# Gate and up projections of 16 of a block's 22 chunks as seven products of quarters over normed activations

## The chip, the cores and the metric

The kernel runs on one core of a Trainium2 chip, in one launch. The metric is the time on the device in microseconds; the time before is 2031.37 us, the median of three runs (2030.7 to 2033.73).

## The reference, cut to what matters

A trunk of two layers over 512 tokens of width 1024, all in float32. Each layer is a feed-forward block, a mixer (layer 0: two kinds of attention, layer 1: a gated delta rule) and a second feed-forward block, so there are four feed-forward blocks. The change touches these:

```
def rms_norm(x, w):
    y = x * rsqrt(mean(x * x, axis=-1) + 1e-6)
    return y * w

def swiglu(h, w_gate, w_up, w_down):
    return (silu(h @ w_gate) * (h @ w_up)) @ w_down

x = x + 0.5 * swiglu(rms_norm(x, ffn_norm), w_gate, w_up, w_down)   # 512 x 1024; weights 1024 x 2816, 2816 x 1024
```

## The kernel before, in words

Activations lie transposed: `self.x` is eight tiles of 128 features by 512 tokens. Every float32 product is made of three matmuls on a high part and a low part of each operand (`mm3`, lines 179 to 183): high by high, high by low, low by high. A weight panel of 128 x 1024 is loaded from SP's queue (`panel`, line 170), its high part is a cast on ScalarE (line 174) and its low part a subtraction on VectorE (line 175). There are three buffers for raw panels and three each for high and low parts (`NRAW, NSPL`).

The norm is split. `prenorm` makes high and low parts of x times the gain (`self.xn`, line 250); the reciprocal root of each token is computed beside the first projections and stands as `self.rb`, the same row on all partitions (line 299). It is multiplied in behind the projection.

`ffn` (line 379) walks the 2816 hidden columns in 22 chunks of 128, in two blocks of 12 and 10. In a block it takes two chunks at a time: `proj_pair` for the gate and one for the up columns, each with two weight panels (half of K, 256 columns), into two PSUM tiles of 128 x 512. Behind it gate and up are each multiplied by rb on VectorE (lines 392, 396), the gate goes through silu on ScalarE, the product is formed (line 398) and split into a high and a low part (lines 226, 227), which stay in one of 14 `hid` tiles. After a block `add_out` multiplies its chunks by the rows of the down weights and adds half of the result to x (line 375). The last block of the network turns x to token order first (`to_tokens`) and adds there (`add_tok`).

Matmuls of the value projection in the attention layer (`proj_tok`, line 348) have 256 moving columns instead of 512, each with its own weight load.

The order on each engine is set by a planner at build time, which takes what is ready by its own model of time; on the chip each engine then works through its queue in that order. Tiles of one tag share a fixed number of buffers, and an instruction that writes a new one waits for the last reader of the old.

Of the kernel before, what the change touches and what calls it, by code (L numbers as in the profile page):

```python
# [10 lines left out]
F32 = mybir.dt.float32  # L11
F32R = mybir.dt.float32r
AF = mybir.ActivationFunctionType
ALU = mybir.AluOpType

P = 128
T = 512
D = 1024
KC = D // P
# [8 lines left out]
NRAW, NSPL = 3, 3  # L28
# [5 lines left out]
ORDER = (0, 1, 2, 3)  # L34
W_DIFF, W_SB = 2, 3
QD = 5
NHID = 14
HDPAD, HIDPAD = 112, 0
TANH = ((0, 0), (2, 0), (1, 1), (0, 1))
PLAN = (  # L40
    ("setup", 0, 3.5, 5), ("decays", 0, 22, 0), ("prep", 0, 25.5, 2.1), ("turned", 0, 43.5, 1.82),
# [60 lines left out]
class Trunk:  # L102
# [129 lines left out]
    def prenorm(self, gain, src=None, wait=1):  # L232

        nc = self.nc
        if src:
            self.xn = [[self.xp.tile([P, T], F32R, tag=f"xn{p}{c}", name=f"xn{p}{c}")
                        for p in "hl"] for c in range(KC)]
            for hf, half in enumerate(src):  # L240
                s = slice(hf * 256, (hf + 1) * 256)
                for c in range(KC):
                    h, l = self.xn[c]
                    self.split_to(h[:, s], l[:, s], half[c], gain[:, c:c + 1])
                    if c % 2:
                        nc.scalar.copy(out=self.x[c][:, s], in_=half[c])
                    else:
                        nc.vector.tensor_copy(self.x[c][:, s], half[c])
        else:
            self.xn = [self.split(self.xp, f"xnh{c}", f"xnl{c}", self.x[c], gain[:, c:c + 1])  # L250
                       for c in range(KC)]
        acc = self.np_.tile([P, T], F32, tag="acc", name="acc", bufs=1)
        nc.scalar.activation(acc, self.x[0], AF.Square)
        for c in range(1, KC):
            sq = self.np_.tile([P, T], F32, tag="sq", name="sq")
            nc.scalar.activation(sq, self.x[c], AF.Square)
            nc.vector.tensor_tensor(acc, acc, sq, op=ALU.add)
        self.pending = ([lambda: None] * wait
                        + [lambda: self.norm_cols(acc), lambda: self.norm_rows()])
# [117 lines left out]


    def ffn(self, wg, wu, wd, first=False, last=None):
        nc = self.nc  # L380
        with ExitStack() as st:
            pool = st.enter_context(self.tc.tile_pool(name="ffn", bufs=2))
            f0 = 0
            for size in (12, 10):
                hid = []
                for f in range(f0, f0 + size, 2):
                    g = self.proj_pair(wg, f * P, (self.a_ps, self.b_ps) if f == 2 else None,
                                       2 if first and f == 0 else 1)
                    u = self.proj_pair(wu, f * P, (self.a_ps, self.b_ps))
                    for j in range(2):  # L390
                        gr = pool.tile([P, T], F32, tag="gr", name="gr")
                        nc.vector.tensor_tensor(gr, g[j], self.rb, op=ALU.mult)  # L392
                        sg = pool.tile([P, T], F32, tag="sg", name="sg")
                        self.last_act = nc.scalar.activation(sg, gr, AF.Silu)
                        ur = pool.tile([P, T], F32, tag="ur", name="ur")
                        nc.vector.tensor_tensor(ur, u[j], self.rb, op=ALU.mult)
                        hd = pool.tile([P, T + HDPAD], F32, tag="hd", name="hd")[:, :T]
                        nc.vector.tensor_tensor(hd, sg, ur, op=ALU.mult)  # L398
                        slot = (f + j) % NHID
                        both = pool.tile([P, 2 * T + HIDPAD], F32R, tag=f"hid{slot}", name=f"hid{slot}",  # L400
                                         bufs=1)
                        h, l = both[:, :T], both[:, T:2 * T]
                        self.split_to(h, l, hd)
                        hid.append((h, l))
                if last is not None and f0 == 0:
                    self.to_tokens(pool)
                if last is None:
                    self.add_out(hid, wd, f0 * P, 0.5, (self.a_ps, self.a_ps, self.b_ps, self.b_ps))
                else:
                    self.add_tok(hid, wd, f0 * P, 0.5, f0 and self.finish(pool, *last))  # L410
                f0 += size

    def to_tokens(self, pool):
        nc = self.nc
        self.xt = []
        for b in range(NB):
            t = pool.tile([P, D], F32, name=f"xt{b}", bufs=1)
            for hf in range(2):
                ps = self.a_ps()
                for c in range(4):  # L420
                    nc.tensor.transpose(out=ps[:, c * P:(c + 1) * P],
                                        in_=self.x[hf * 4 + c][:, b * P:(b + 1) * P],
                                        identity=self.ident)
                nc.vector.tensor_copy(t[:, hf * 512:(hf + 1) * 512], ps)
            self.xt.append(t)
# [778 lines left out]
```

## Time and profile before

| | before |
|---|---|
| time, median of 3 runs | 2031.37 us (2030.7 to 2033.73) |
| profiled execution, its own time | 2032.96 us |
| its span | 2031.2 us |
| TensorE, VectorE, ScalarE, GpSimd busy | 1999.0, 1084.6, 748.3, 130.9 us |
| transfers | 192.24 MB, 95 GB/s |

The profile is of one execution. PE is TensorE's matmuls, PEld its weight loads, DVE VectorE, ACT ScalarE, POOL GpSimd; SPq and ACTq are queues that issue transfers. Line numbers are those of the kernel before. A row of the timeline has the start, the duration and what ran; matmuls are shown longer than the distance between their starts, since they are pipelined and their ends are modelled.

### The profile page before, as it was taken

Reading aid. Unit: us, or ns where it says so; the run is one execution under the profiler, and the core shown is the slowest. Engines: PE = TensorE matmul, PEld = TensorE weight load, DVE = VectorE, ACT = ScalarE, POOL = GpSimd, SP = SyncE. Lnnn points to the kernel's source line nnn. Section 1 sums busy time; section 2 is a strip of 40 time slices with the busy share of each in tenths; the row PEclk is TensorE's granted clock in tenths of the full one; section 3 lists DMA queues with packets and bytes.
Section 4 is the critical chain, followed back from the end, with each engine's and each line's share of the span. In section 5 each row is a group of like instructions: output and inputs, shape, how many; then the busy total and the mean of one; then the engine's idle time right before and its main releaser. Section 6 shows DMA issues by size and latency. Waiting matters only on the chain.

```text
span 2031.2 us, 24843 instructions
## 1 busy us (share of the span) xinstructions
PE 1999.0 (98%) x9786; PEld 1667.5 (82%) x9786; DVE 1084.6 (53%) x1752; ACT 748.3 (37%) x1359; POOL 130.9 (6%) x298
## 2 busy tenths in 40 slices
PE   8999999999999999999999999998999999999998
PEld 7888888889888888888888888877877788888887
DVE  6452454597675433444544344478577685443543
ACT  5232233355663222233332232355465453322322
POOL 0000000100000000000000000005432400000000
PEclk9999999999999999999999999999999999999999
DMA  4333333222123333333333333234223233223332
GB/s 157 94 99 98 94 99 98 86 84 73 47 90 103 94 104 94 94 103 94 94 95 102 94 95 103 93 111 115 77 80 92 75 100 104 94 90 97 93 101 76
DMA packets 189866, 192.24 MB, mean 95 GB/s; under 512 B 28546, under 2 KB 165044, under 8 KB 189748
## 3 DMA queue, kind: packets, MB, share of 16 engines
q1 hardware_dynamic: 158916, 182.62, 28.7%
q10 hardware_dynamic: 30832, 8.02, 1.7%
q8 instruction: 77, 1.26, 0.3%
q14 instruction: 41, 0.34, 0.1%
HBM read 185.35 MB, written 5.26 MB: 94 GB/s over the span
## 4 chain that ended last, share of the span: by engine, by line
PE 89%; POOL 5%; DMA 2%; DVE 1%; issue 1%; ACT 1%; ACTq 0%; SPq 0%; POOLq 0%
PE mm L181 10%; PE mm L182 10%; PE mm L183 10%; PE pa L181 9%; PE pa L183 8%; PE pa L182 8%; PE pb L181 8%; PE pb L183 8%; PE pb L182 8%; PE mm L96 4%; POOL tmp L1037 2%; POOL rr L1040 2%; PE pb L96 1%; DMA lb<-iud 1%; DMA iud<-iu 1%
## 5 line engine op out<-in xcount | busy, mean ns | idle before, releaser
L175 DVE TENSOR_TENSOR wl<-raw,wh 128x1024 fp32r<-128x1024 f32 (+1 forms) x348 | 413.2, 1187 | 564.1 <-ACT wh L174 563.1
L174 ACT CAST wh<-raw 128x1024 fp32r<-128x1024 f32 (+1 forms) x348 | 355.6, 1022 | 702.0 <-PE pb L182 279.9
L181 PE MATMUL mm<-xnh,wh 128*128 128x512 f32 (+1 forms) x816 | 316.5, 389 | 0.6 <-ACT wh L174 0.6
L183 PE MATMUL mm<-xnh,wl 128*128 128x512 f32 (+1 forms) x816 | 317.1, 389 | 0.0
L182 PE MATMUL mm<-xnl,wh 128*128 128x512 f32 (+1 forms) x816 | 316.7, 388 | 0.0
L181 PEld LDWEIGHTS mm<-xnh,wh 128*128 128x128 f32 x816 | 154.3, 189 | 31.6 <-ACT wh L174 1.0
L183 PEld LDWEIGHTS mm<-xnh,wl 128*128 128x128 f32 x816 | 154.2, 189 | 30.5 <-issue 0.5
L182 PEld LDWEIGHTS mm<-xnl,wh 128*128 128x128 f32 x816 | 154.3, 189 | 30.4 <-issue 0.2
L181 PE MATMUL pa<-xnh,wh 128*128 128x512 f32 x400 | 156.2, 390 | 0.0
L183 PE MATMUL pa<-xnh,wl 128*128 128x512 f32 x400 | 155.8, 389 | 0.0
L183 PE MATMUL pb<-xnh,wl 128*128 128x512 f32 x400 | 155.7, 389 | 0.0
L181 PE MATMUL pb<-xnh,wh 128*128 128x512 f32 x400 | 155.7, 389 | 0.0
L182 PE MATMUL pa<-xnl,wh 128*128 128x512 f32 x400 | 155.7, 389 | 0.0
L182 PE MATMUL pb<-xnl,wh 128*128 128x512 f32 x400 | 155.7, 389 | 0.0
L226 ACT CAST hid<-hd 128x512 fp32r<-128x512 f32 x88 | 54.5, 620 | 209.0 <-DVE hd L398 209.0
L96 PE MATMUL mm<-xnh,wh 128*128 128x512 f32 x256 | 109.2, 426 | 12.0 <-DVE cx L926 12.0
L392 DVE TENSOR_TENSOR gr<-mm,rb 128x512 f32<-128x512 f32 x80 | 55.2, 691 | 94.7 <-PE mm L183 94.6
L183 PE MATMUL pb<-hid,wl 128*128 128x512 f32 x264 | 102.8, 389 | 0.0
L181 PE MATMUL pa<-hid,wh 128*128 128x512 f32 x264 | 102.7, 389 | 0.0
L182 PE MATMUL pa<-hid,wh 128*128 128x512 f32 x264 | 102.7, 389 | 0.0
L183 PE MATMUL pa<-hid,wl 128*128 128x512 f32 x264 | 102.7, 389 | 0.0
L181 PE MATMUL pb<-hid,wh 128*128 128x512 f32 x264 | 102.7, 389 | 0.0
(308 smaller groups left out, 3365.1 us busy)
## 6 DMA issues: line engine op xcount, KB each, us to landing
raw<-in_ffn_w_gate_dram SPq DMA_DIRECT2D x88, 512.0 KB, 3.6
raw<-in_ffn_w_up_dram SPq DMA_DIRECT2D x88, 512.0 KB, 3.6
raw<-in_ffn_w_down_dram SPq DMA_DIRECT2D x88, 512.0 KB, 3.6
raw<-in_gdn_w_in_dram SPq DMA_DIRECT2D x32, 512.0 KB, 3.9
raw<-in_att_w_in_dram SPq DMA_DIRECT2D x24, 512.0 KB, 3.5
raw<-in_gdn_w_out_dram SPq DMA_DIRECT2D x16, 256.0 KB, 2.7
xr<-in_x_dram SPq DMA_DIRECT2D x4, 512.0 KB, 5.6
raw<-in_att_w_out_dram SPq DMA_DIRECT2D x4, 512.0 KB, 3.4
```

Of the source, the lines that this page charges most:

```text
L96: return self.tc.keep_in_program_order(self.engine.matmul(*args, **kw))
L174: nc.scalar.copy(out=h[:, :n], in_=raw[:, :n])
L175: nc.vector.tensor_tensor(l[:, :n], raw[:, :n], h[:, :n].bitcast(F32), op=ALU.subtract)
L181: self.te.matmul(out, lhsT=lh, rhs=rh, start=start, stop=False)
L182: self.te.matmul(out, lhsT=lh, rhs=rl, start=False, stop=False)
L183: self.te.matmul(out, lhsT=ll, rhs=rh, start=False, stop=stop)
L226: nc.scalar.copy(out=h, in_=src)
L392: nc.vector.tensor_tensor(gr, g[j], self.rb, op=ALU.mult)
L1037: nc.gpsimd.tensor_tensor(p, rr[:, :k, j:j + 1].broadcast_to(sh), lb[:, j, j + 1:].rearrange("p (o m) -> p o m", o=1) .broadcast_to(sh), o ...
L1040: nc.gpsimd.tensor_tensor(rr[:, :k, j + 1:], rr[:, :k, j + 1:], p, op=ALU.subtract)
```

## The change

In three of the four feed-forward blocks (all but the last) the 22 chunks are taken as 6, 8 and 8 instead of 12 and 10. The first six go as before (`eight`). Beside the down projection of these six, `quarters` multiplies x by gain and rb into normed activations, cuts them into quarters (half of K by half of the tokens) and keeps the high and low parts of the seven left operands, 28 tiles, in the tiles of `self.xn` and 12 more. The other 16 chunks go through `seven`, two chunks a time: the gate and up weights of the two chunks are cut into quarters (half of K by one chunk), and seven products of 256 tokens replace eight. Sums of quarters of weights come from transfers that add to what the tile holds (issued from GpSimd, `accum_op`) and from VectorE (t2, t4). Sums of products form partly in PSUM, where a second product adds to a first (X, Y, Z), partly on VectorE. The result is normed already, so the multiplications by rb fall away on this path. The hidden tiles are 10 instead of 14. The last block keeps 12 and 10 chunks and 14 tiles.

```diff
     def ffn(self, wg, wu, wd, first=False, last=None):
-        nc = self.nc
+        nc = self.nc
+        sizes, ring = ((12, 10), 14) if last is not None else ((6, 8, 8), 10)
         with ExitStack() as st:
             pool = st.enter_context(self.tc.tile_pool(name="ffn", bufs=2))
             f0 = 0
-            for size in (12, 10):
+            for size in sizes:
                 hid = []
                 for f in range(f0, f0 + size, 2):
-                    g = self.proj_pair(wg, f * P, (self.a_ps, self.b_ps) if f == 2 else None,
-                                       2 if first and f == 0 else 1)
-                    u = self.proj_pair(wu, f * P, (self.a_ps, self.b_ps))
-                    for j in range(2):
-                        gr = pool.tile([P, T], F32, tag="gr", name="gr")
-                        nc.vector.tensor_tensor(gr, g[j], self.rb, op=ALU.mult)
-                        sg = pool.tile([P, T], F32, tag="sg", name="sg")
-                        self.last_act = nc.scalar.activation(sg, gr, AF.Silu)
-                        ur = pool.tile([P, T], F32, tag="ur", name="ur")
-                        nc.vector.tensor_tensor(ur, u[j], self.rb, op=ALU.mult)
-                        hd = pool.tile([P, T + HDPAD], F32, tag="hd", name="hd")[:, :T]
-                        nc.vector.tensor_tensor(hd, sg, ur, op=ALU.mult)
-                        slot = (f + j) % NHID
-                        both = pool.tile([P, 2 * T + HIDPAD], F32R, tag=f"hid{slot}", name=f"hid{slot}",
+                    if f0 and last is None:
+                        inner = self.seven(pool, wg, wu, f)
+                    else:
+                        inner = self.eight(pool, wg, wu, f, first)
+                    for j, hd in enumerate(inner):
+                        slot = (f + j) % ring
+                        both = pool.tile([P, 2 * T], F32R, tag=f"hid{slot}", name=f"hid{slot}",
                                          bufs=1)
-                        h, l = both[:, :T], both[:, T:2 * T]
+                        h, l = both[:, :T], both[:, T:]
                         self.split_to(h, l, hd)
                         hid.append((h, l))
-                if last is not None and f0 == 0:
-                    self.to_tokens(pool)
+                if f0 == 0:
+                    if last is None:
+                        self.quarters(pool)
+                    else:
+                        self.to_tokens(pool)
                 if last is None:
                     self.add_out(hid, wd, f0 * P, 0.5, (self.a_ps, self.a_ps, self.b_ps, self.b_ps))
                 else:
                     self.add_tok(hid, wd, f0 * P, 0.5, f0 and self.finish(pool, *last))
                 f0 += size
+    def small(self, pool, tag):
+        n = T + HDPAD if tag == "hd" else T
+        return pool.tile([P, n], F32, tag=tag, name=tag)[:, :T]
+    def eight(self, pool, wg, wu, f, first):
+        nc = self.nc
+        g = self.proj_pair(wg, f * P, (self.a_ps, self.b_ps) if f == 2 else None,
+                           2 if first and f == 0 else 1)
+        u = self.proj_pair(wu, f * P, (self.a_ps, self.b_ps))
+        for j in range(2):
+            gr, sg, ur, hd = (self.small(pool, t) for t in ("gr", "sg", "ur", "hd"))
+            nc.vector.tensor_tensor(gr, g[j], self.rb, op=ALU.mult)
+            self.last_act = nc.scalar.activation(sg, gr, AF.Silu)
+            nc.vector.tensor_tensor(ur, u[j], self.rb, op=ALU.mult)
+            nc.vector.tensor_tensor(hd, sg, ur, op=ALU.mult)
+            yield hd
+    def quarters(self, pool):
+        nc = self.nc
+        tags = [(self.xp, f"xn{p}{c}") for c in range(KC) for p in "hl"]
+        tags += [(pool, f"sx{i}") for i in range(12)]
+        norm = []
+        for kh in range(2):
+            t = pool.tile([P, 4 * T], F32, tag="sr", name="xr")
+            for k in range(4):
+                c = kh * 4 + k
+                nc.vector.scalar_tensor_tensor(t[:, k * T:(k + 1) * T], self.x[c],
+                                               self.gain[:, c:c + 1], self.rb, ALU.mult, ALU.mult)
+            norm.append(t.rearrange("p (k t) -> p k t", k=4))
+        self.left = [[[], []] for _ in range(7)]
+        v2 = lambda t: t.rearrange("p (k t) -> p k t", k=2)
+        for i in range(2):
+            a = [[norm[kh][:, 2 * i:2 * i + 2, t * 256:(t + 1) * 256] for kh in range(2)]
+                 for t in range(2)]
+            s1, s2, s3, s4 = (v2(self.small(pool, t)) for t in ("gr", "sg", "ur", "hd"))
+            tt = nc.vector.tensor_tensor
+            tt(s1, a[1][0], a[1][1], op=ALU.subtract)
+            tt(s2, s1, a[0][0], op=ALU.subtract)
+            tt(s3, a[0][0], a[1][0], op=ALU.subtract)
+            tt(s4, a[0][1], s2, op=ALU.add)
+            for o, src in enumerate((a[0][0], s2, s1, s3, a[0][1], a[1][1], s4)):
+                h, l = (v2(pl.tile([P, T], F32R, tag=tag, name=tag, bufs=1))
+                        for pl, tag in (tags.pop(0), tags.pop(0)))
+                self.split_to(h, l, src)
+                self.left[o][0].append(h)
+                self.left[o][1].append(l)
+    def seven(self, pool, wg, wu, f):
+        nc = self.nc
+        x8 = lambda t: t.rearrange("p (x c) -> p x c", x=8)
+        def load(eng, v, kh, lo, hi, **kw):
+            for q, w in enumerate((wg, wu)):
+                eng.dma_start(v[:, q * 4:q * 4 + 4], w[kh * 512:(kh + 1) * 512,
+                                                       f * P + lo:f * P + hi]
+                              .rearrange("(k p) c -> p k c", p=P), **kw)
+        raw = lambda: x8(self.wp.tile([P, 1024], F32, tag="raw", name="raw", bufs=NRAW))
+        add = dict(accum_op=ALU.add)
+        b11 = x8(pool.tile([P, 1024], F32, tag="sb", name="sb"))
+        load(nc.sync, b11, 0, 0, P)
+        b2 = x8(pool.tile([P, 2048], F32, tag="sr", name="sr"))
+        load(nc.sync, b2, 1, 0, 2 * P)
+        t1, t3 = raw(), raw()
+        load(nc.sync, t1, 0, 0, P)
+        load(nc.gpsimd, t1, 0, P, 2 * P, **add)
+        load(nc.sync, t3, 0, P, 2 * P)
+        load(nc.gpsimd, t3, 1, P, 2 * P, **add)
+        b21, b22 = b2[:, :, :P], b2[:, :, P:]
+        X, Y, Z = self.mm_ps(), self.a_ps(), self.b_ps()
+        def product(ps, o, right, start=False):
+            h = x8(self.wp.tile([P, 1024], F32R, tag="wh", name="wh", bufs=NSPL))
+            l = x8(self.wp.tile([P, 1024], F32R, tag="wl", name="wl", bufs=NSPL))
+            self.split_to(h, l, right)
+            ah, al = self.left[o]
+            for q in range(2):
+                out = ps[:, q * 256:(q + 1) * 256]
+                for k in range(4):
+                    a = [t[k // 2][:, k % 2] for t in (ah, al)]
+                    for i, (wt, xt) in enumerate(((h, a[0]), (h, a[1]), (l, a[0]))):
+                        nc.tensor.matmul(out, lhsT=wt[:, q * 4 + k], rhs=xt,
+                                         start=start and q + k + i == 0,
+                                         stop=q == 1 and k == 3 and i == 2, skip_group_check=True)
+        def combine(tag, a, b, op):
+            t = self.small(pool, tag)
+            nc.vector.tensor_tensor(t, a, b, op=op)
+            return t
+        product(X, 0, b11, True)
+        p1 = self.np_.tile([P, T], F32, tag="acc", name="p1", bufs=1)
+        nc.scalar.copy(out=p1, in_=X)
+        t2 = raw()
+        nc.vector.tensor_tensor(t2, t1, b22, op=ALU.add)
+        product(Y, 1, t2, True)
+        u2 = self.np_.tile([P, T], F32, tag="sq", name="u2")
+        nc.vector.tensor_tensor(u2, p1, Y, op=ALU.add)
+        product(Z, 2, t1, True)
+        product(Y, 3, t3)
+        u3 = self.np_.tile([P, T], F32, tag="sq", name="u3")
+        nc.vector.tensor_tensor(u3, p1, Y, op=ALU.add)
+        c22 = combine("gr", Z, u3, ALU.subtract)
+        product(X, 4, b21)
+        t4 = raw()
+        nc.vector.tensor_tensor(t4, t2, b21, op=ALU.add)
+        product(Y, 5, t4)
+        c21 = combine("ur", p1, Y, ALU.add)
+        product(Z, 6, b22)
+        c12 = combine("ur", Z, u2, ALU.subtract)
+        for lo, hi in ((X, c21), (c12, c22)):
+            sg, hd = self.small(pool, "sg"), self.small(pool, "hd")
+            for i, c in enumerate((lo, hi)):
+                s = slice(i * 256, (i + 1) * 256)
+                self.last_act = nc.scalar.activation(sg[:, s], c[:, :256], AF.Silu)
+                nc.vector.tensor_tensor(hd[:, s], sg[:, s], c[:, 256:], op=ALU.mult)
+            yield hd
 
     def to_tokens(self, pool):
         nc = self.nc
```

## Rows read from the trace of the kernel before

**Rows 1.** The page, part 1: busy time, share of the span, instructions of each engine.
```profile
PE 1999.0 (98%) x9786; PEld 1667.5 (82%) x9786; DVE 1084.6 (53%) x1752; ACT 748.3 (37%) x1359; POOL 130.9 (6%) x298
```

**Rows 2.** The page, part 4: the chain that ended last, by engine.
```profile
PE 89%; POOL 5%; DMA 2%; DVE 1%; issue 1%; ACT 1%; ACTq 0%; SPq 0%; POOLq 0%
```

**Rows 3.** Busy time by stretch, the second feed-forward of layer 0 and what follows.
```profile
core 0: us, PE busy (x) PEld busy (x) DVE busy (x) ACT busy (x) POOL busy (x), PEclk, DMA share, GB/s
...
620.00:980.00 360.00, 360.00 (x1593) 298.16 (x1592) 161.22 (x191) 105.69 (x127) 1.87 (x1) 1.00 0.32 98
```

**Rows 4.** Timeline of TensorE, 512 columns: start, duration, what; 33 steps between.
```profile
140.12 0.39 PE L181 MATMUL pb<-xnh,wh 128*128 128x512 f32 x1
...
147.60 0.39 PE L181 MATMUL pa<-hid,wh 128*128 128x512 f32 x1
```

**Rows 5.** Timeline of TensorE, 256 columns, a projection's first and last of 96.
```profile
399.30 0.28 PE L181 MATMUL mm<-wh,xnh 128*128 128x256 f32 x1
399.30 0.19 PEld L182 LDWEIGHTS mm<-wl,xnh 128*128 128x128 f32 x1
...
410.69 0.28 PE L183 MATMUL mm<-wh,xnl 128*128 128x256 f32 x1
```

**Rows 6.** Groups by line: names, shapes, count | busy us, mean ns | idle before, releaser.
```profile
L175 DVE TENSOR_TENSOR wl<-raw,wh 128x1024 fp32r<-128x1024 f32 x324 | 396.7, 1224 | 557.6 <-ACT wh L174 556.6 <-DMA raw<-in_gdn_w_in_dram 0.4
L174 ACT CAST wh<-raw 128x1024 fp32r<-128x1024 f32 x324 | 340.7, 1052 | 677.1 <-PE pb L182 279.9 <-PE mm L182 149.3 <-issue 139.4
...
L227 DVE TENSOR_TENSOR hid<-hd,hid 128x512 fp32r<-128x512 f32 x88 | 60.8, 691 | 54.3 <-ACT hid L226 54.2
L398 DVE TENSOR_TENSOR hd<-sg,ur 128x512 f32<-128x512 f32 x88 | 60.5, 688 | 2.2 <-ACT sg L394 0.8
...
L394 ACT ACTIVATE sg<-gr 128x512 f32<-128x512 f32 x88 | 55.2, 628 | 128.7 <-DVE gr L392 128.7
L226 ACT CAST hid<-hd 128x512 fp32r<-128x512 f32 x88 | 54.5, 620 | 209.0 <-DVE hd L398 209.0
...
L396 DVE TENSOR_TENSOR ur<-pa,rb 128x512 f32<-128x512 f32 x44 | 30.4, 690 | 23.9 <-PE pa L183 23.9
L230 DVE SCALAR_TENSOR_TENSOR xnl<-x,norms,xnh 128x512 fp32r<-128x512 f32 x40 | 29.9, 753 | 0.4
...
L620 DVE TENSOR_TENSOR s<-pb,bias 128x256 f32<-128x256 f32 x8 | 3.3, 412 | 0.3 <-PE pb L617 0.3
```

**Rows 7.** Timeline of VectorE where the first block's down projection begins (147.60).
```profile
147.80 0.69 DVE L396 TENSOR_TENSOR ur<-pb,rb 128x512 f32<-128x512 f32 x1
148.70 1.23 DVE L175 TENSOR_TENSOR wl<-raw,wh 128x1024 fp32r<-128x1024 f32 x1 [0.21 <-ACT wh L174]
149.84 0.68 DVE L398 TENSOR_TENSOR hd<-sg,ur 128x512 f32<-128x512 f32 x1
```

**Rows 8.** Waits of SP's queue, 20 to 370 us: in total, times, longest.
```profile
SPq L170 <- DVE wl L175: 319.0, 64, 10.9
```

**Rows 9.** Transfers: issues, KB each, median us from issue to landing.
```profile
raw<-in_ffn_w_gate_dram SPq DMA_DIRECT2D x88, 512.0 KB, 3.6
...
lb<-iud ACTq DMA_DIRECT2D x16, 128.0 KB, 3.5
r<-rd ACTq DMA_DIRECT2D x8, 256.0 KB, 2.9
```

**Rows 10.** Waits of VectorE, 20 to 370 us: in total, times, longest.
```profile
DVE gr L392 <- PE mm L183: 23.6, 18, 2.0
DVE hid L227 <- ACT hid L226: 13.7, 20, 0.7
DVE ur L396 <- PE pa L183: 6.0, 10, 0.6
```

More of the change, by code (lines that the diff above doesn't have):

```diff
@@ L36 @@
 QD = 5
-NHID = 14
-HDPAD, HIDPAD = 112, 0
+HDPAD = 112
 TANH = ((0, 0), (2, 0), (1, 1), (0, 1))
@@ L232, in prenorm @@
     def prenorm(self, gain, src=None, wait=1):
-        nc = self.nc
+        nc, self.gain = self.nc, gain
         if src:
```

## The prediction

> **What bounds the kernel now.** I read the engine line of the page first [rows 1]: TensorE is busy 1999.0 of 2031.2 us, VectorE 1084.6, ScalarE 748.3, GpSimd 130.9. Then the chain that ended last [rows 2]: 89% of it is TensorE, so whatever shortens TensorE's stream shortens the kernel, until another engine's queue is late. Then the feed-forward stretches alone [rows 3]: TensorE is busy without a gap at full granted clock (1.00, the 2.4 GHz level), VectorE 161.2 of 360 us, the transfers take 0.32 of their engines' time at 98 GB/s. The busy time of one matmul is no price, since matmuls overlap in the record; the price is the distance between starts. For 512 columns [rows 4] 33 steps take 147.60 - 140.12 = 7.48 us, 0.2267 us each. For 256 columns, which the value projection of the attention layer already uses with a new weight load for each, the 96 matmuls of one projection [rows 5] have 95 steps in 410.69 - 399.30 = 11.39 us, 0.1199 each. That is more than half of 0.2267 (0.1133): halving a matmul costs 6%, and the change halves them.
>
> **TensorE's part of the change.** A pair of chunks (256 gate and 256 up columns) costs 2 projections x 2 x 8 x 3 = 96 matmuls of 512 columns now: 96 x 0.2267 = 21.76 us. By seven products it costs 7 x 2 x 4 x 3 = 168 of 256 columns: 168 x 0.1199 = 20.14 us. The gain is 1.62 us a pair (7.4%, where seven eighths would be 12.5%). Three of the four blocks take this path, eight pairs each: 24 x 1.62 = 38.9 us. The down projection keeps its matmuls, 6 + 8 + 8 chunks in place of 12 + 10.
>
> The Trainium skill (TensorE: Matmul & The Clock Gate, Back-to-back issue gap) prices a lone warm gap at the columns over 2.4 GHz plus 2.5 ns, 215.8 and 109.2 ns; as an estimate this would make a pair 20.72 and 18.35 us and the gain 24 x 2.37 = 57 us. The trace disagrees with both gaps (227 and 120 ns), and with the same section's 131 ns for a sustained stream of 512 columns; the measured gaps decide, and the sum stays at 38.9.
>
> **VectorE beside a pair.** Durations from [rows 6]. It now makes seven low parts of 1024 columns instead of four, adds two sums t2 and t4 of that size (9 x 1.224 = 11.0 us), five combinations of 512 that read PSUM (5 x 0.690 = 3.5), four products of 256 (nearest the 256-column addition, 4 x 0.412 = 1.6) and two low parts of the hidden tiles (2 x 0.691 = 1.4): 17.5 us in 20.14. The multiplications by rb behind the projections are gone. Back to back the pieces overlap a little (148.70 to 149.84 is 1.14 us for a piece shown with 1.23 [rows 7]), about 0.08 on each of 20 pieces, so 15.9 to 17.5 us, 79 to 87%. ScalarE: seven casts of 1.052, a copy and two casts of 0.620, four halves of a 0.628 activation at most: 11.7 us. Both fit. What is behind whom: with three buffers for high and low parts, the parts of a product can be made once the third product before it is done; two products, 2 x 24 x 0.1199 = 5.75 us, cover one cast and one subtraction of 2.28, which leaves 3.4 us of slack for VectorE's order. Product four writes the bank that u2 has read, with one product (2.88 us) in between. I charge 0.3 us a pair, 7.2 in all: bounds 0 (the gapless stretches now) and 1.4 (rival A).
>
> **The transfers.** A pair loads 2 MiB now and 3.5 MiB then: four operands of 0.5 MiB in 512-byte rows, the second half of K whole (1 MiB), and t1 and t3 brought by an accumulating transfer each. 3.67 MB in 20.14 us is 182 GB/s; by the 0.32 share for 98 GB/s [rows 3] that is 0.59 of the engines' time, if accumulating costs as loading does. Issued from SP: eight a pair instead of four; SP now waits for VectorE to give buffers back (319.0 us in 64 waits of one block, [rows 8]), so loads start early enough with room left. The accumulating ones stand on GpSimd's queue, which has nothing else in these stretches; each waits for the plain load before it. This is the part that no row shows. One tile needs two of 256 KB. Lower end: both at once as one 512 KB load, 3.6 us; upper end: in turn at the rate of the slowest load, 128 KB in 3.5 us, so 14.0 [rows 9]. I take the 256 KB load in 512-byte rows, twice in turn, 5.8 us, since its rows are of the same size. The cover: t1 of the next pair gets its buffer when t4 has been made, some 3.5 us after a pair's start (the low part of product two at 2.3, then t4), and the parts of the next pair's product one must be ready 8 x 2.88 = 23.0 us after that start. Taking off the sum t2, a cast and a subtraction (3.5), 16.0 us are left for the load (3.6) and the accumulation. 5.8 fits; above 12.4 TensorE waits even with perfect order.
>
> **The quarters.** Once a block VectorE makes eight normed tiles (0.753), eight sums (0.688) and 14 low parts (0.691), 6.0 + 5.5 + 9.7 = 21.2 us, and ScalarE 14 casts, 8.7 us. They stand beside the down projection of six chunks, 144 x 0.2267 = 32.6 us, with that projection's six panels (7.3), the rest of the last pair (ur, hd and two hidden parts, 4.1), four updates of x (2.8) and the first parts of the seven products (4.9): 40.3 us, 7.7 too many. But the order is not the program's: at 148.70 a panel of the down projection is split between pieces of an earlier pair [rows 7], so ready work is moved ahead, and the normed tiles need only x and rb, known early in the block. Without them the overhang is 1.7. I charge 2 us a block, 6 in all (0 to 24). The eight further updates of x a block, 5.5 us, lie beside the down panels, where VectorE is under half busy; without that cover 16.5 us.
>
> **Sum.** The profiled execution took 2032.96 us, 1.6 over the median of 2031.37. 2032.96 - 38.9 + 7.2 + 6.0 = 2007.3; beside the median 2005.7, so I say **2006 us**. Own range 1992 (no stalls) to 2026 (quarters at 24, pairs at 0.3 and a little more).
>
> **Rivals.** A: VectorE becomes the bound. For it: its queue is in order, and in a block it now waits 23.6 + 13.7 + 6.0 us for TensorE and ScalarE beside panels [rows 10], over 11 pairs 3.9 us a pair. 17.5 + 3.9 = 21.4 us, gain 0.3 a pair, 8 in all, less the quarters: 2030. Against: much of that waiting is for work that isn't due. 18%; it goes from 2024 to 2038.
>
> B, slower: an accumulating transfer lands late at the head of VectorE's queue. t2 waits for it there, and u2, u3 and the low parts of products in progress stand behind it. The planner places t2 by its own idea of that transfer; what lands over 3.4 us after its place stops TensorE, every pair. The gain is gone at a wait of 1.37 us a pair (1.62 less a block's 2 us over eight), 4.8 us late. With the transfer at 10.6 us, between the 5.8 taken and the 14.0, and a place chosen by 3.6, it is 7.0 late: 3.6 us of wait, pair 23.74, 24 x 1.98 + 6 = 54 slower, 2085; at 14.0 it is 2167. For it: no accumulating transfer or GpSimd issue is in the trace. Against: the 16.0 us of cover. 24%.
>
> The Trainium skill (Collectives: The Full Stack, The bandwidth ceiling) says that an adding transfer runs at half the rate because it needs two source reads; as an estimate 7.2 us for 512 KB. No run here shows it; by it the tile lands 3.6 us late and the wait is 0.2 us, still a gain.
>
> C: a matmul of 256 columns doesn't keep its pace. The weight load is shown with 0.19 us; if it bound, a pair would take 168 x 0.19 = 31.9 us and the kernel 243 more, 2275. [rows 5] are against it: 0.1199 with a load each. 2%.
>
> **How the numbers follow.** Forecast 56%, A 18%, B 24%, C 2%. About 0.2% (4 us) is what can be told from no change. Faster: 55 of the forecast and 5 of A, 0.60; same: 9 of A, 1 of the forecast, 1 of B, 0.11; slower: 4 of A, 23 of B, 2 of C, 0.29. The range 1990 to 2062 holds nearly all of the forecast and A and some two fifths of B, about 82%.
>
> **What would show it.** Steps of 0.12 us between the 256-column matmuls and 20.1 to 20.5 us from one pair to the next would show the main term; TensorE gaps inside pairs, ended by VectorE's low parts, rival A; VectorE's t2 waiting for the accumulating transfer, rival B, with the landing times of the transfers issued from GpSimd as its measure. Gaps in the down projection of the first six chunks would price the quarters. The forecast is wrong if pairs take over 21.4 us, or if the transfers' share passes 0.9.

## The result, and the profile after

The changed kernel takes **2076.86 us** (median of 4 runs, 2076.05 to 2081.11) against 2031.89 for the kernel before on the same chip: a ratio of **1.0225, 95% interval 1.0207 to 1.0242**. It is 45 us slower; the forecast was 26 us faster, with a range that ended at 2062. The profiled execution took 2081.11 us, 48.1 over the one of before.

The page of the changed kernel answers to [rows 1] and [rows 2]: the span, the busy times, two DMA queues (packets, MB, share of 16 engines' time; q0 carries the accumulating transfers), the chain that ended last.

```profile
span 2079.3 us, 29425 instructions
...
PE 1992.8 (96%) x11514; PEld 1741.8 (84%) x11514; DVE 1302.3 (63%) x2058; ACT 897.7 (43%) x1577; POOL 256.0 (12%) x394
...
q1 hardware_dynamic: 209604, 195.21, 30.7%
q0 software_dynamic: 50688, 25.17, 9.9%
...
PE 53%; DMA 6%; POOL 5%; DVE 3%; issue 2%; ACT 1%; ACTq 0%; DVEq 0%; POOLq 0%; SPq 0%
```

The 53% can't be set beside the 89% of before. The shares of this chain add up to some 70% of the span, because it could be followed back only to 607.6 us; of the part followed, about three quarters are TensorE's. What the chain does show is DMA: 6% of the span, about 8% of the part followed, where it was 2%. TensorE now waits, and behind the wait stands a transfer. Nor has TensorE's busy time fallen by the 39 us of the sum: 1999.0 to 1992.8. ScalarE's has risen by 149 us; 41 of these (32 loads of activation tables, below) are in no term of the sum.

The waits of the changed kernel (engine and tile, what ended the wait: us in all, times, longest):

```profile
DVE raw L511 <- DMA raw<-in_ffn_w_up_dram: 70.5, 21, 5.3
...
PE pa L498 <- DVE u L518: 38.2, 17, 3.8
```

L511 is the sum t2, L518 the combination u3, L498 the seven products. VectorE waits at t2 for an accumulating transfer, and TensorE waits for u3. The chain of waits links the two, in one pair of the second layer (start, duration, what):

```profile
755.94 2.88 PE mm L498 x24
...
762.74 1.24 DVE wl L226
...
763.98 0.68 POOL raw L471
764.65 0.08 issue
764.73 5.90 DMA raw<-in_ffn_w_up_dram
...
770.80 1.23 DVE raw L511
772.03 0.61 DVE u L518
772.64 0.14 issue
772.77 4.61 PE pa L498 x24
```

And VectorE's timeline of the same pair (line 522 is the sum t4, which gives back the buffer that t1 of the next pair takes):

```profile
759.07 1.22 DVE L522 TENSOR_TENSOR raw<-raw,sr 128x1024 f32<-128x1024 f32 x1
...
765.62 1.22 DVE L226 TENSOR_TENSOR wl<-raw,wh 128x1024 fp32r<-128x1024 f32 x1 [1.66 <-ACT wh L225]
770.80 1.23 DVE L511 TENSOR_TENSOR raw<-raw,sr 128x1024 f32<-128x1024 f32 x1 [3.96 <-DMA raw<-in_ffn_w_up_dram]
771.95 0.68 DVE L518 TENSOR_TENSOR u<-p,pa 128x512 f32<-128x512 f32 x1
```

The t2 at 770.80 belongs to the **next** pair, whose product two begins at 783.12, 12 us on. In VectorE's queue it stands ahead of this pair's u3. Its operand lands at 770.63, VectorE stands idle for 3.96 us, and u3, which needs product four, is made only at 771.95, 4.5 us after the last matmul of that product began (767.41). Product six writes the bank that u3 reads, so TensorE stops between products five and six.

Windows of the changed kernel around that stop, and over the attention layer (busy us of each engine, then PEclk, DMA share, GB/s; the share counts the whole time of every packet that starts in the window, so it can pass 1 in a short one):

```profile
core 0: us, PE busy (x) PEld busy (x) DVE busy (x) ACT busy (x) POOL busy (x), PEclk, DMA share, GB/s
386.50:636.50 250.00, 236.45 (x1331) 202.78 (x1330) 174.25 (x376) 168.87 (x333) 9.82 (x12) 0.97 0.23 71
...
734.60:824.30 89.70, 84.27 (x674) 83.75 (x673) 63.22 (x76) 39.29 (x53) 15.63 (x12) 0.96 0.70 158
...
767.20:770.20 3.00, 3.00 (x27) 2.93 (x25) 0.00 (x0) 1.05 (x1) 1.99 (x2) 1.00 1.30 159
770.20:772.80 2.60, 0.16 (x3) 0.06 (x1) 2.00 (x3) 1.33 (x2) 0.00 (x0) 1.00 1.30 161
772.80:777.40 4.60, 4.60 (x26) 4.60 (x27) 3.36 (x5) 0.47 (x2) 0.00 (x0) 0.63 0.57 176
777.40:780.20 2.80, 2.80 (x25) 2.80 (x25) 2.25 (x3) 1.32 (x2) 0.00 (x0) 1.00 0.98 277
```

A second price shows here. After 2.4 us of idling, the granted clock of the next 4.6 us is 0.63 on the mean, mostly the 1.2 GHz level, and product six takes 4.61 us where the others take 2.88. By the starts of the 24 matmuls behind each of the 18 stops, 11 were followed so (4.3 to 5.3 us), 7 were not (2.9).

**Where the time went.** I measured the six stretches of four pairs (672 matmuls each) from the starts of their matmuls. At 0.12 us a step each is 80.63 us, 483.8 in all, where the old path takes 6 x 4 x 21.76 = 522.2. After the change they take 88.57, 95.33, 89.71, 90.47, 90.90 and 90.59, 545.6 in all. The excess of 61.8 us is 42.3 of gaps (one in each of the first three pairs of a stretch, steps of 1.1 to 4.1 us, mean 2.5) and 19.5 of longer steps behind them. The attention layer, read apart from the pairs that follow it, takes 250.1 us in place of 228.0: 22.1 more. The projections before and after it, in the other layers, differ by some 2 us. Together -38.4 + 61.8 + 22.1 + 2 = +47.5, of the 48.1 seen.

The attention layer is a cost of its own. ScalarE's groups there, by line:

```profile
L813 ACT ACT_TABLE_LOAD x14 | 18.0, 1283 | 0.2
...
L823 ACT ACT_TABLE_LOAD x9 | 11.5, 1283 | 0.2
...
L812 ACT ACT_TABLE_LOAD x5 | 6.4, 1283 | 0.1
```

These are 28 loads of activation tables of 1.283 us, 36 us of ScalarE, at the exponentials (812, 823) and the logarithm (813); the whole kernel has 40 loads, and had 8. (The expectation below counts 29, with one at line 623.) The same stretch before, in a window of that kernel:

```profile
376.10:604.00 227.90, 227.90 (x1330) 199.02 (x1329) 175.06 (x381) 132.03 (x305) 10.92 (x19) 1.00 0.23 73
```

The same matmuls, gapless then; now TensorE idles 13.5 us and ScalarE has 37 us more. The other 8.6 of the 22.1 us are TensorE's busy time (236.45 in place of 227.90), at a granted clock of 0.97 in place of 1.00: here too the stops are followed by slower matmuls. The timeline of ScalarE at the end of the block before shows where it starts:

```profile
338.50 0.41 ACT L531 ACTIVATE sg<-gr 128x256 f32<-128x256 f32 x1
338.92 1.28 ACT L187 ACT_TABLE_LOAD   x1
...
341.29 1.28 ACT L531 ACT_TABLE_LOAD   x1
342.58 0.42 ACT L531 ACTIVATE sg<-ur 128x256 f32<-128x256 f32 x1
```

Line 187 loads a table that holds both exponential and logarithm, pinned behind `self.last_act`, the last silu that the program wrote. On the new path that is c22's, which is ready before those of c21 and c12 (`ur`). So the load goes in at 338.92, a late silu at 341.29 brings its own table back, and from then on the attention layer fetches a table at many changes between exponential and logarithm.

### The profile page after: what moved, and what is told of

Read it like the earlier page. It is cut to its first block, busy times and chain, and to the rows that moved or that the text cites. A ratio compares the mean times of both kernels' runs of the same rounds, so it can differ in the third digit from the quotient of the medians.

```text
span 2079.3 us, 29425 instructions
## 1 busy us (share of the span) xinstructions
PE 1992.8 (96%) x11514; PEld 1741.8 (84%) x11514; DVE 1302.3 (63%) x2058; ACT 897.7 (43%) x1577; POOL 256.0 (12%) x394
## 3 DMA queue, kind: packets, MB, share of 16 engines
q0 software_dynamic: 50688, 25.17, 9.9%
## 4 chain that ended last, share of the span: by engine, by line
PE 53%; DMA 6%; POOL 5%; DVE 3%; issue 2%; ACT 1%; ACTq 0%; DVEq 0%; POOLq 0%; SPq 0%
PE pa L498 5%; PE pa L182 5%; PE pa L180 5%; PE pa L181 5%; PE pb L182 5%; PE pb L180 5%; PE pb L181 5%; PE mm L95 4%; DMA raw<-in_ffn_w_up_dram 4%; PE pb L498 3%; PE mm L498 3%; PE mm L181 3%; PE mm L180 3%; PE mm L182 3%; POOL tmp L1159 2%; POOL rr L1162 2%
## 5 line engine op out<-in xcount | busy, mean ns | idle before, releaser
L174 DVE TENSOR_TENSOR wl<-raw,wh 128x1024 fp32r<-128x1024 f32 (+1 forms) x252 | 295.5, 1173 | 275.2 <-ACT wh L173 274.4
L173 ACT CAST wh<-raw 128x1024 fp32r<-128x1024 f32 (+1 forms) x252 | 254.3, 1009 | 425.6 <-PE pb L181 153.5
L180 PE MATMUL mm<-xnh,wh 128*128 128x512 f32 (+1 forms) x432 | 169.3, 395 | 7.7 <-DVE qT L660 5.6
L182 PE MATMUL mm<-xnh,wl 128*128 128x512 f32 (+1 forms) x432 | 169.9, 394 | 0.0
L181 PE MATMUL mm<-xnl,wh 128*128 128x512 f32 (+1 forms) x432 | 168.8, 391 | 0.0
L226 DVE TENSOR_TENSOR wl<-raw,wh 128x1024 fp32r<-128x1024 f32 x96 | 117.5, 1224 | 73.2 <-ACT wh L225 73.2
L471 POOL DMA_DIRECT2D raw<-in_ffn_w_gate_dram x48 | 67.8, 1412 | 698.0 <-DMA raw<-in_ffn_w_gate_dram 330.0
L498 PE MATMUL pa<-xnh,wh 128*128 128x256 f32 x288 | 87.0, 302 | 39.5 <-DVE u L518 38.2
L498 PE MATMUL pa<-sx,wh 128*128 128x256 f32 x576 | 118.0, 298 | 0.0
L181 PE MATMUL pb<-hid,wh 128*128 128x512 f32 x264 | 102.7, 389 | 0.0
L180 PE MATMUL pb<-hid,wh 128*128 128x512 f32 x264 | 102.2, 389 | 0.0
L95 PE MATMUL mm<-xnl,wh 128*128 128x512 f32 x256 | 101.8, 398 | 0.0
L95 PE MATMUL mm<-xnh,wl 128*128 128x512 f32 x256 | 101.7, 397 | 0.0
L498 PEld LDWEIGHTS pa<-sx,wh 128*128 128x128 f32 x576 | 97.5, 208 | 0.0
```

Of the source, the lines that this page charges most:

```text
L95: return self.tc.keep_in_program_order(self.engine.matmul(*args, **kw))
L173: nc.scalar.copy(out=h[:, :n], in_=raw[:, :n])
L174: nc.vector.tensor_tensor(l[:, :n], raw[:, :n], h[:, :n].bitcast(F32), op=ALU.subtract)
L180: self.te.matmul(out, lhsT=lh, rhs=rh, start=start, stop=False)
L181: self.te.matmul(out, lhsT=lh, rhs=rl, start=False, stop=False)
L182: self.te.matmul(out, lhsT=ll, rhs=rh, start=False, stop=stop)
```

## The experiments

My theory: the two losses are independent. The first: t2 at the head of VectorE's queue holds u3, through its place and not through a lack of room on VectorE. The second: the table load, pinned behind the wrong silu, costs the attention layer 22 us. The rivals: VectorE is simply too full (A of the prediction); the transfers are too slow, so that no order helps; and, for the attention layer, the extra traffic or the shifted schedule.

**The table load behind all four silus.** `acts` takes the place of `last_act` at both silus.

```diff
-        self.tc.add_manual_dep(ld.ins, self.last_act.ins.name, dep, reason="tables")
+        for act in self.acts[-4:]:
+            self.tc.add_manual_dep(ld.ins, act.ins.name, dep, reason="tables")
```

> The attention layer's stretch became 22 us longer although none of its code changed: ScalarE loads its activation tables 29 times there instead of once (1.283 us each, 36 us more of ScalarE). Theory: the table load of that layer waits for the activation that the program issues last in the feed-forward block, and on the new path this is no longer the one that runs last, so a silu behind it brings its own table back. Here the load waits for the last four silus; nothing else changes. My theory: at most two loads in that layer's stretch, TensorE's idle time of 13.5 us there gone, 22 us less, 2055 (2050 to 2060); the stretches of seven products stay at 88 to 95 us. Rival (the layer is late because of buffers or transfers left over from the block before): loads go, time stays within 5 us of 2077.

Measured: 2061.60 us (2057.58 to 2065.7, 4 runs), ratio 1.0147 (1.0130 to 1.0164). The kernel's loads fall from 40 to 10, and the part from the start of the attention layer to the down projection behind it from 315.4 to 293.7 us, 21.7 less. One load is left in that layer, and it stands behind the last silu (ScalarE's timeline of this kernel):

```profile
347.96 0.41 ACT L533 ACTIVATE sg<-ur 128x256 f32<-128x256 f32 x1
348.39 1.28 ACT L188 ACT_TABLE_LOAD   x1
```

The second theory holds, and nothing else moved on VectorE and TensorE: both have the same instructions in the same order as in the changed kernel. The time fell by only 15.3 us, to 1.6 above the 2060 that I had allowed. In this profile the six stretches came out 4.5 us longer (550.1), which the edit does not explain, and its runs spread over 8 us; the profiled execution of the changed kernel was also the slowest of its four, 4.3 us over their median.

**Without the accumulating transfers.**

```diff
-        load(nc.gpsimd, t1, 0, P, 2 * P, **add)
...
-        load(nc.gpsimd, t3, 1, P, 2 * P, **add)
```

> Left out: the accumulating transfers, so that t1 and t3 hold one quarter of the weights each instead of a sum. Everything else is issued as before. Theory (the accumulating transfer lands late and what stands behind it on VectorE stops TensorE): the gap of 1.1 to 4.1 us in three of four pairs goes, and with it the half clock behind it; a stretch of four pairs takes 81 to 83 us instead of 88.6 to 95.3, in all some 58 us less, 2019 (2010 to 2028). Rival A (VectorE has too much work): stretches stay above 87 us, time above 2060.

Measured: 2017.76 us, ratio 0.9931 (0.9917 to 0.9946). All six stretches take 80.63 us, without a gap; the attention part stays at 315.4. The order of the instructions on TensorE, VectorE and ScalarE is that of the changed kernel; only the transfers are gone. So VectorE has room for everything that the pairs give it, and rival A falls. What is left adds up: 2031.5 - 38.4 + 22.1 + 2 = 2017.2.

**t2 behind the previous pair's u3.** Nothing is taken away; the edit has two entries of VectorE's queue change places.

```diff
-        nc.vector.tensor_tensor(t2, t1, b22, op=ALU.add)
+        with self.tc.issue_after(self.u3) if self.u3 else nullcontext():
+            nc.vector.tensor_tensor(t2, t1, b22, op=ALU.add)
...
-        nc.vector.tensor_tensor(u3, p1, Y, op=ALU.add)
+        self.u3 = nc.vector.tensor_tensor(u3, p1, Y, op=ALU.add).ins
```

> Only the order of two instructions on VectorE changes: the next pair's sum t2, which waits for the accumulating transfer, goes behind u3 instead of ahead of it, in three of four pairs. Same work, same transfers. Theory (head of the queue): u3 is done on time, product six of seven starts without a gap, the clock stays; the tile still lands before product one of the next pair needs it. Stretches 81 to 84 us, 2022 (2012 to 2035). Rival (the chain of load and accumulation is too long whatever the order): the gap moves to the next pair's first products, time above 2060. Rival A (too much work on VectorE): also above 2060.

Measured: 2035.67 us (10 runs), ratio 1.0020 (1.0011 to 1.0030): 41 us back from the 2076.86, yet just above the range that I expected. The stretches take 83.1 to 83.8 us (500.6 in all). The gap at product six is gone. Smaller ones, steps of 0.56 to 1.4 us, stand in product seven: ahead of its first matmul, and a little later where its low part is first needed. VectorE and TensorE in one of them, this kernel's timeline:

```profile
774.79 1.23 DVE L513 TENSOR_TENSOR raw<-raw,sr 128x1024 f32<-128x1024 f32 x1 [3.93 <-DMA raw<-in_ffn_w_up_dram]
775.94 0.68 DVE L505 TENSOR_TENSOR gr<-pb,u 128x512 f32<-128x512 f32 x1
776.54 1.21 DVE L227 TENSOR_TENSOR wl<-sr,wh 128x1024 fp32r<-128x1024 f32 x1
...
776.77 0.36 PE L499 MATMUL pb<-xnh,wh 128*128 128x256 f32 x1 [1.12 <-DVE gr L505]
777.81 0.39 PE L499 MATMUL pb<-xnh,wl 128*128 128x256 f32 x1 [0.33 <-DVE wl L227]
```

t2 waits as long as before (3.93 us), but now c22 (line 505) and the low part of product seven stand behind it, which are due later. The exchange is not a clean one: the planner also put c22 ahead of that low part, and in the first three pairs of a stretch two matmuls of the next pair's product one inside product seven. The window over this stop has the clock at 1.00, so nothing is paid twice:

```profile
772.00:775.50 3.50, 3.50 (x31) 3.45 (x29) 0.70 (x1) 1.33 (x2) 1.01 (x1) 1.00 1.23 151
775.50:780.50 5.00, 3.55 (x28) 3.23 (x27) 5.00 (x8) 1.67 (x3) 0.00 (x0) 1.00 0.64 108
```

**Both together.** The two diffs above.

> Both of the other two edits together: table load behind the last four silus, t2 behind u3. If the two costs are separate they add: 2077 - 22 - 55 = 2000 (1990 to 2013), faster than the kernel before by some 32 us, near the 2006 that the sum of the prediction gave. If one of them only hid the other, the two gains don't add and it stays above 2020.

Measured: 2013.46 us (2010.74 to 2016.79), ratio 0.9911 (0.9896 to 0.9925). The two effects add, as independent losses must: the attention part gains 21.7 us, as with the tables alone, and the stretches 46.8, where the new order alone gained 45.0. They take 498.8, 15 us over the ideal, and these are the 13 us over my 2000. One place further back was not far enough.

**t2 behind all that is urgent: behind the previous pair's c21,** with the tables mended.

```diff
+            self.made = nc.vector.tensor_tensor(t, a, b, op=op).ins
...
+        with self.tc.issue_after(self.u3) if self.u3 else nullcontext():
+            nc.vector.tensor_tensor(t2, t1, b22, op=ALU.add)
...
         c21 = combine("ur", p1, Y, ALU.add)
+        self.u3 = self.made
```

> As the version with both edits (2013), but the next pair's t2 stands behind c21, the combination after product six, instead of behind u3. With u3 ahead alone the stretches keep gaps of 0.6 to 1.4 us at products six and seven of the second and third pair, in all 15 us over six stretches. Theory: while VectorE waits for the tile at t2, the low parts of products six and seven stand behind it; behind c21 nothing waits, so stretches take 80.6 to 81.5 us and the time is 2000 (1995 to 2006). Rival (t2 is now too late itself): a gap at product two of the next pair, stretches at 82 us or more.

Measured: **1996.95 us** (1995.76 to 1997.9), ratio **0.9826 (0.9812 to 0.9841)**, 35 us under the kernel before and, with the next version, the fastest of all. (The gaps that u3 ahead alone had left were all in product seven, none in six.) Every stretch takes 80.63 us, and TensorE's instructions stand in the order of the changed kernel. The windows of a stretch and of the down projection of six chunks ahead of it, and t2 with what precedes it in VectorE's timeline, all of this kernel:

```profile
657.10:689.80 32.70, 32.70 (x146) 27.05 (x146) 23.11 (x32) 10.71 (x16) 5.26 (x4) 1.00 0.71 162
689.80:770.40 80.60, 80.60 (x673) 80.60 (x672) 63.27 (x76) 39.00 (x53) 15.66 (x12) 1.00 0.78 174
```

```profile
727.41 0.69 DVE L506 TENSOR_TENSOR ur<-p,pa 128x512 f32<-128x512 f32 x1
728.01 1.22 DVE L514 TENSOR_TENSOR raw<-raw,sr 128x1024 f32<-128x1024 f32 x1
```

t2 starts right behind c21 with no idling: by then the tile has landed. The transfers are no faster (their share of the engines' time is 0.78, and the accumulating ones land after 5.3 and 6.4 us by the median, 4.9 and 6.3 in the changed kernel). So the rival "too slow for any order" falls too.

**t2 on GpSimd,** with the tables mended: the wait goes to a queue where nothing urgent stands.

```diff
-        nc.vector.tensor_tensor(t2, t1, b22, op=ALU.add)
+        nc.gpsimd.tensor_tensor(t2, t1, b22, op=ALU.add)
```

> Table load behind the last four silus, and t2 made on GpSimd instead of VectorE; the accumulating transfers stay. Theory (what hurts is the place in VectorE's queue, not the chain): the wait for the tile moves to GpSimd's queue, where only the transfers of the next pair stand behind it; stretches 80.6 to 83 us, time 2001 (1995 to 2012). Rival (GpSimd's sum of two tiles in SBUF holds up VectorE's subtractions, or takes over 6 us): low parts of 1024 columns go from 1.22 us to over 1.5, stretches above 84 us.

Measured: 1997.72 us (1995.72 to 1998.34), ratio 0.9832 (0.9815 to 0.9848); 80.63 us a stretch. Another engine, the same result, as the first theory says. It has a price that this kernel can hide, by the groups by line:

```profile
L513 POOL TENSOR_TENSOR raw<-raw,sr 128x1024 f32<-128x1024 f32 x24 | 62.6, 2607 | 30.3 <-DVE wl L228 15.2 <-DMA raw<-in_ffn_w_up_dram 8.1 <-issue 6.9
...
L228 DVE TENSOR_TENSOR wl<-sb,wh 128x1024 fp32r<-128x1024 f32 x24 | 58.8, 2451 | 48.7 <-ACT wh L227 48.7
```

The sum takes 2.61 us on GpSimd (1.22 on VectorE), and VectorE's low part of `sb`, which stands beside it, takes 2.45 us on the mean, 1.22 in the version before this one.

**No accumulating transfers, the sums t1 and t3 on GpSimd,** with the tables mended: the first half of K comes whole, 2 MiB a pair, and the four loads of t1 and t3 go.

```diff
-        load(nc.sync, b11, 0, 0, P)
+        load(nc.sync, b1, 0, 0, 2 * P)
...
+        nc.gpsimd.tensor_tensor(t1, b11, b12, op=ALU.add)
+        nc.gpsimd.tensor_tensor(t3, b12, b22, op=ALU.add)
```

> Table load behind the last four silus; no accumulating transfers: the first half of K is loaded whole once (2 MiB a pair instead of 3.5) and GpSimd adds the quarters for t1 and t3. t2 stays on VectorE. Theory (the chain of load and accumulating load is what is late): the sums read tiles that are loaded a pair ahead, t1 is there as soon as its buffer is free plus one sum; gaps under 0.3 us, stretches 80.6 to 82, share of the transfer engines in them from 0.65 to 0.35, time 2000 (1994 to 2010). Rival (GpSimd's sums are slow or hold up VectorE): stretches above 84 us and VectorE's 1024-column pieces above 1.5 us.

Measured: 2003.87 us (2002.55 to 2005.81), ratio 0.9862 (0.9847 to 0.9876); the stretches take 492.3, 8.5 over the ideal. With less than two thirds of the bytes it is slower than the version that accumulates. The groups of this kernel, and VectorE's timeline where product four of a second pair starts 0.26 us late (143.87):

```profile
L228 DVE TENSOR_TENSOR wl<-sr,wh 128x1024 fp32r<-128x1024 f32 x48 | 88.7, 1847 | 0.5
L485 POOL TENSOR_TENSOR raw<-sb 128x1024 f32<-128x1024 f32 x24 | 76.3, 3178 | 613.8 <-DVE wl L175 317.5 <-ACT p L510 179.3 <-issue 62.5
```

```profile
140.32 2.90 DVE L228 TENSOR_TENSOR hid<-hd,hid 128x512 fp32r<-128x512 f32 x1
143.14 0.68 DVE L515 TENSOR_TENSOR u<-p,pa 128x512 f32<-128x512 f32 x1
```

The first of GpSimd's two sums takes 3.18 us, and VectorE's low parts of `sr` 1.85 on the mean instead of 1.22. In the timeline a low part of 512 columns takes 2.90 us (0.68 at 137.11, before GpSimd begins) while GpSimd adds (139.40 to 145.47), u2 comes behind it, and product four waits for u2. The steps that are too long are of this kind: some 0.38 us from start to start (0.66 once), at products four and six of the second and third pair of a stretch. That all 8.5 us come from GpSimd's sums is not shown by a run of its own. The chain that ended last has 7% of VectorE, 2% where every stretch was gapless (the version behind c21).

**GpSimd's transfers overwrite instead of adding.** One run.

```diff
-        load(nc.gpsimd, t1, 0, P, 2 * P, **add)
+        load(nc.gpsimd, t1, 0, P, 2 * P)
...
-        load(nc.gpsimd, t3, 1, P, 2 * P, **add)
+        load(nc.gpsimd, t3, 1, P, 2 * P)
```

> Only the adding is left out of the transfers issued from GpSimd: they overwrite the tile instead (t1 and t3 then hold one quarter, not a sum); order and waits are the kernel's after the change. It tells the price of adding from that of issuing from GpSimd. If adding costs (two reads), landing falls from 4.9 and 6.3 us (gate and up) to about 4 and 5, the queue's time per MB from 131 us of one engine to near the 52 of SP's queue, and the gaps of 1.1 to 4.1 us shrink below 1. If issuing costs, landing and gaps stay within 0.5 us of what they are, time 2070 to 2080.

Measured: 2036.59 us; the stretches take 501.9. Its page and its transfers (the last number is the median us from issue to landing):

```profile
q0 software_dynamic: 7680, 25.17, 4.4%
...
raw<-in_ffn_w_gate_dram POOLq DMA_DIRECT2D x48, 256.0 KB, 4.1
raw<-in_ffn_w_up_dram POOLq DMA_DIRECT2D x48, 256.0 KB, 4.1
```

The changed kernel's, by its transfers:

```profile
raw<-in_ffn_w_gate_dram POOLq DMA_DIRECT2D x48, 256.0 KB, 4.9
raw<-in_ffn_w_up_dram POOLq DMA_DIRECT2D x48, 256.0 KB, 6.3
```

The same bytes from the same queue, and the same order on TensorE, VectorE and ScalarE: adding makes 50688 packets where there were 7680, and lands up to 2.2 us later. The gaps shrink to steps of 0.48 to 1.76 us, not all below the 1 us that I expected, and 43.7 of the 61.8 us are gone. So the addition is what turned a small delay into a large one; the order of the queue is what makes it a delay at all.

## Why the prediction was wrong

**Right: TensorE's part.** 38.9 us was the gain in the sum, and 80.63 us a stretch in three kernels makes it 522.2 - 483.8 = 38.4. The 256-column pace of [rows 5] holds, so rival C falls.

**Right in sign, too dear: the quarters.** The down projection beside which they are made takes 32.64 us in every block, 144 x 0.2267. I charged 6 us; they cost nothing. VectorE is busy for 23.1 of the 32.7 us of that window, where I had counted 40.3 us of work: part of it stands well ahead of the window, the eight normed tiles at 617.46 to 622.84 and the first sums of quarters from 647.06 on (the kernel with t2 behind c21).

**Right: VectorE and ScalarE fit.** 63.27 of 80.60 us in the gapless stretch shown is 78%, just under my 79 to 87. Rival A, to which I gave 18%, does not hold: the stretches without the wait have no gap.

**Nearly right: the transfers' time.** From t4's end (759.07 + 1.22) to the first accumulating issue (763.98) it took 3.7 us, and the accumulating pair 6.65, from 763.98 to 770.63; I had 3.6 and 5.8. The chain puts the end of the 3.7 us down to a low part on VectorE (762.74 + 1.24), so the plain load may have landed a little sooner. The tile landed 14.9 us after the pair's first matmul (755.77), well ahead of its own use. The 16.0 us of cover were real. The Trainium skill (Collectives: The Full Stack, The bandwidth ceiling) has the adding step of a ReduceScatter at half the rate of a copy, because the add reads two sources; the prediction carried this over to a load into SBUF. The trace agrees roughly: the share of q0 times 16 engines times the span, over 25.17 MB, is 131 us of engine time per MB when adding and 57 when not, 2.3 times.

**Wrong: "I charge 0.3 us a pair, 7.2 in all".** This is the step that failed: it measured 61.8. I took cover from an operand's need, and an in-order queue takes it from the operand's **place**. Rival B said just this and had 24%, because I set "the 16.0 us of cover" against it, an argument about need. Its slack was wrong too: "over 3.4 us after its place" is the slack of the low parts, but the entry behind t2 was u3. In the pair shown t2's place was reached at 766.84 and product six was due at 770.17, 0.12 us after product five's last matmul began (770.05). Taking off u3 with its handover (772.77 - 771.95 = 0.82) and t2 itself (771.95 - 770.80 = 1.15) leaves 768.20, only 1.4 us after the place; t2 started at 770.80, 2.6 us past that, which is the gap. I had noted that product four writes the bank that u2 has read, with one product in between. Product six and u3 are the same pattern, and there I did not look at who stands ahead in the queue.

**Wrong: the clock left out of the price.** Neither the charge nor rival B's 2085 held the 19.5 us that matmuls lost behind the gaps, nearly all at the 1.2 GHz level. That B's 2085 comes near the measured time is luck: its wait was 3.6 us in all 24 pairs, the measured one 2.4 on the mean in 18 (42.3 us), plus the clock, plus a cost that B did not have.

**Missed: the tables, 22.1 us.** The diff moves the line that sets `last_act` into a loop over (X, c21) and (c12, c22), and the order in which these are ready is not the order in which they are written. Nothing in the profile of before points at it, but the diff does: it moves that name, and a helper elsewhere in the kernel pins an instruction to it.

With both mended, which is another kernel than the one forecast, the sum holds: 1996.95 lies in its own range of 1992 to 2026, 9 us under 2006. The charges of 7.2 and 6.0 were not needed there, some 3 us went to other layers (2032.3 - 38.4 = 1993.9), and 0.9 is by how much the kernel before itself took longer beside it (2032.3).

## What to carry to other kernels

On an in-order queue, count an operand's lateness from the place of the instruction that waits for it, and ask of each instruction behind it how little time it has; an early operand's slack does not help the neighbour. Put a wait of uncertain length behind the last urgent entry, or on a queue that has none. Where a diff reorders work, look for every name that other code uses as "the last one".

## What was not expected of the hardware

- A stop of a few us in a stream at full clock was often paid twice: 11 of 18 were followed by matmuls at the 1.2 GHz level (product six 4.61 us in place of 2.88, granted clock 0.63). Behind the 16 stops of the kernel that overwrites (steps of 0.48 to 1.76 us), none was; the 24 matmuls took 2.95 us each time.
- An accumulating transfer of 256 KB in 512-byte rows landed after 4.9 to 6.3 us, a plain one from the same queue after 4.1, with 6.6 times fewer packets. Its issue is dearer as well: the groups of the changed kernel show 1412 ns on GpSimd for the gate weights and 1917 for the up weights, those of the overwriting one 754 and 748.
- GpSimd's sums of two tiles in SBUF slowed VectorE's subtractions beside them from 1.22 to 2.45 us on the mean. The Trainium skill (SBUF — State Buffer, Who interferes with whom) says that a VectorE instruction with two inputs in SBUF contends with GpSimd's reads; the rows above agree.
- A load of an activation table took 1.283 us of ScalarE on the mean, 28 times in one attention layer. TensorE's granted clock over that layer was 0.97, and 1.00 before.
